# Product order at group ends, residuals and token sums around the second norm, and own buffers for later modulation chunks, in a one-core diffusion block

## The chip, the core and the metric

The kernel runs on one core of a Trainium2 chip. Its engines are TensorE (PE; its weight loads are shown as PEld), VectorE (DVE), ScalarE (ACT), GpSimd (POOL) and SyncE (SP), which issues most DMAs on one in-order queue. The metric is the device time of one execution in microseconds, the median of several runs.

## The reference

One layer of a hybrid backbone on 512 latent tokens of width 2048, with 256 context tokens that only feed the states of the scans. All is in 32-bit floats. Cut to what matters:

```python
mod = c_act @ w_mod + b_mod                 # six vectors of 2048: shift, scale, gate, twice
h = rmsnorm(x, g_norm1) * (1 + sc1) + sh1
z = h @ w_in                                # 4 GLA heads and 4 mLSTM heads: q, k, v, gates
x = x + gt1 * merge_groups(gla(z), mlstm(z), gates, w_out)
h2 = rmsnorm(x, g_norm2) * (1 + sc2) + sh2
u_gate, u_val = split(h2 @ w_up)            # 2 x 5504
g = conv3x3_depthwise(u_gate on an 8 x 64 grid) + conv_b
x = x + gt2 * ((silu(g) * u_val) @ w_down)
out = rmsnorm(x, g_final)
```

## The kernel before

Activations lie transposed: 16 tiles of 128 channels by 512 tokens. Every large product is made of three: a 32-bit operand is split into a high part that ScalarE casts (L89) and a low remainder that VectorE subtracts (L90), and `mm3` adds high x high, high x low and low x high. `load_split` brings a block of weights (128 x 1024 floats, 512 KB) by a DMA on SP's queue into one of four raw buffers (`wraw`, L166) and splits it into one of two high and two low buffers. PSUM has six large banks (`acc`) and two small ones (`psb`) that turn.

The stages follow each other so:

- Projections for the eight heads, those of heads 0 and 1 together at the start; after that, while head h is scanned (`stages`: GLA for h below 4, mLSTM above), the projection for head h+1 runs in between (`project_steps`, 8 loads), and the mixture is written out by hand through `weave`: a stage yields the number of microseconds that it wants covered and gets as many steps of products. While the last head is scanned, the first gate unit (`ga0`) takes the projection's place. TensorE's order in these stages is the program's. In an mLSTM head the products `pg` come first, each in a small bank that ScalarE's exponentials (tile `ed`, L829) read; GpSimd cuts triangles out of `ed` (L832, the selects); then come `cst`, `s` and `po`, whose results are evicted as `dn` and `ob`.
- Three more gate units (`ga1` to `ga3`) and four output units (`wo`), each of 8 loads, 4 blocks and 96 matmuls for a block.
- The second norm: `residual` adds gate x product to x (L957), `square` squares on ScalarE (L964) and adds into a running sum on VectorE, the last two tiles staying apart; `token_rstd` adds these sums over the channels with matmuls against a column of ones (`ps_rms`, L976), takes the root and spreads it (`rb_rms`, L983).
- The up and down projections. Four of the 43 blocks of 128 features run as plain products (`up_two`, tile `u`); the other 39 by `up_seven`: seven products of half size in place of eight, in banks `x`, `w` and `v`. Product 6 of a step is held back as `last` and runs inside the next step, behind its product 0, so that its bank is free by then; at the end of a group it runs at once. After every seventh step or so a group of the down projection (`down_block`, tile `dn`) runs, six in all.
- The last norm, with the same helpers.

Four of the six modulation vectors (regions 2 to 5) aren't needed before the first residual. They are worked out on VectorE, ScalarE and GpSimd beside the products, as a list of fillers that `load_split` takes from: `rate[0]` is added to a credit at each load, and each whole credit takes a filler. For each of 4 regions and 4 blocks, `mod_fillers` lists 8 chunks, 2 empty fillers and an end. A chunk (`mod_chunk`) loads 512 KB (`raw_m`, L248), sums one half on VectorE (L257) and scales the other on ScalarE (L258) for GpSimd to add (L259). The end (`mod_end`, tile `mc`, L268) adds over the channels with four small matmuls in a small bank, in program order on TensorE. `modraw[0]` is the pool that chunks take their tile from: the four weight buffers until the second gate unit, then four tiles of their own. `rate[0]` is 2 on the last five loads of the projections for heads 4 to 7, 2 in the first gate unit and 2.25 after it.

Of the kernel before, what the change touches and what calls it, by code (L numbers as in the profile page):

```python
# [11 lines left out]
F32 = mybir.dt.float32  # L12
# [6 lines left out]
P = 128  # L19
D = 2048  # L20
KT = D // P
# [48 lines left out]
def block_kernel(ctx: ExitStack, tc: tile.TileContext, a: dict, out: bass.AP):  # L70
# [88 lines left out]
    rate, credit = [0], [0]  # L159
    modraw = [wraw]  # L160

# [82 lines left out]
    def mod_chunk(region, n, kp, parts):  # L244

        name = f"m{region}_{n}_{kp}"
        raw = modraw[0].tile([P, 2, T], F32, name=f"raw_{name}", tag="raw")
        nc.sync.dma_start(raw, a["w_mod2"][region - 2, n, kp])  # L248
        if kp == 0:
            parts += [sum_tile(i, name) for i in range(2)]  # L250
        dv, po = parts
        ce, co = (csil[:, 2 * kp + i : 2 * kp + i + 1] for i in range(2))
        if kp == 0:
            V.tensor_scalar(out=dv, in0=raw[:, 0, :], scalar1=ce, scalar2=None, op0=ALU.mult)
            S.activation(po, raw[:, 1, :], AF.Copy, scale=co)  # L255
        else:
            V.scalar_tensor_tensor(out=dv, in0=raw[:, 0, :], scalar=ce, in1=dv, op0=ALU.mult, op1=ALU.add)  # L257
            S.activation(raw[:, 1, :], raw[:, 1, :], AF.Copy, scale=co)  # L258
            G.tensor_tensor(out=po, in0=po, in1=raw[:, 1, :], op=ALU.add)  # L259
        if kp == KP - 1:  # L260
            G.tensor_tensor(out=po, in0=po, in1=dv, op=ALU.add)
# [671 lines left out]
    rp = pool(st_3, "rp")  # L933
    modraw[0] = pool(st_3, "mraw3", 4)
    rate[0] = 2.25
    for g in range(4):
# [22 lines left out]
    def square(k, sums, pl, tag, sl=slice(0, T)):  # L959

        n = sl.stop - sl.start
        first = not sums
        sq = pl.tile([P, n], F32, name=f"sq{tag}{k}", tag=f"{tag}s" if first else f"{tag}{k}" if k >= KT - 2 else tag)
        S.activation(sq, x2[k][:, sl], AF.Square)  # L964
        if first or k >= KT - 2:
            sums.append(sq)
        else:
            add(sums[0], sums[0], sq)

    def token_rstd(sums, pl, name, n=T):  # L970

        nj = n // P
        ps = psb(f"ps_{name}", (P, nj))
        for j in range(nj):
            for i, sq in enumerate(sums):
                PE.matmul(ps[:, j : j + 1], sq[:, P * j : P * j + P], cst[:, C_ONE : C_ONE + 1],  # L976
                          start=(i == 0), stop=(i == len(sums) - 1))
        var, scr, r = (pl.tile([P, nj], F32, name=f"{t}_{name}", tag=t) for t in ("rs1", "rs2", "rs3"))
# [137 lines left out]

    def up_seven(f, pending):

# [28 lines left out]
        pad, val = pads[f % 2], vtile(f)  # L1147
        product(0, a11, x, True)
        with tc.high_priority():
            S.copy(p1, x)  # L1150
        pending()
        product(1, a12, w, True)
        with tc.high_priority():
            add(a11, s1, a11)
            add(a12, a12, a11)
        with tc.high_priority():
            add(pad[:, 1 : ROWS // 2 + 1, 1 : GW + 1], rows(w), rows(p1))
        product(3, s1, v, True)
        with tc.high_priority():
            S.copy(p5, v)  # L1160
        product(2, a11, x, False)
        with tc.high_priority():
            S.copy(u2, x)
        product(5, a12, v, False)
        with tc.high_priority():
            add(pad[:, ROWS // 2 + 1 : ROWS + 1, 1 : GW + 1], rows(v), rows(u2))
        product(4, s3, x, False)
        with tc.high_priority():
            neg_add(val[:, hi], x, p5)

        def last():
            product(6, a22, x, False)
            with tc.high_priority():
                S.activation(val[:, lo], x, AF.Copy, scale=-1.0)
            conv(f, pad, val)

        return last

# [22 lines left out]
    for f in range(FIRST, NF):  # L1201
        last = up_seven(f, last)
        if f == NF - 1 or len(todo) > 1 and f > todo[0][-1]:
            last()
            last = lambda: None
        if len(todo) > 1 and f > todo[0][-1]:
# [144 lines left out]
```

## Time and profile before

| what | us |
|---|---|
| median of three runs (lowest, highest) | 2542.25 (2541.1, 2545.07) |
| the profiled execution's own time | 2540.94 |
| its span, first to last instruction | 2539.2 |
| TensorE busy | 2459.1 |
| VectorE busy | 1666.5 |
| ScalarE busy | 1023.7 |
| GpSimd busy | 301.2 |

The granted clock has a mean of 0.990 over the span. In a row of the trace come start, length, engine, line, operation, tiles (out <- in), shapes and count; in brackets the idle time of the engine before it and what ended that. A row of waits names who waited for what, the total, the number of times and the longest. Matmul ends are modelled, so distances between starts are surer than lengths.

### The profile page before, as it was taken

The page shows a single profiled execution, that of the slowest core. Times are in us where ns is not written, and L with a number is a line of the kernel's source. Part 1 is how long each engine was busy: PE and PEld are TensorE (multiplying, and loading weights), DVE is VectorE, ACT ScalarE, POOL GpSimd, SP SyncE. Part 2 cuts the span into 40 slices and gives each one's busy share as a digit, 9 for nine tenths or more (in the row PEclk, how much of TensorE's full clock was granted, in tenths as well). Part 3 has the DMA queues.
Part 4 walks back from the last instruction along what each step waited for, and adds up shares of the span by engine and source line. Part 5 has one row for each costly group of instructions (what it writes and reads, how often), then busy time and mean ns, then how long its engine had stood idle before and what let it go on. Part 6 is the DMA issues. An engine that isn't in the chain of part 4 may idle for free.

```text
span 2539.2 us, 39245 instructions
## 1 busy us (share of the span) xinstructions
PE 2459.1 (97%) x15758; PEld 2212.8 (87%) x15758; DVE 1666.5 (66%) x2375; ACT 1023.7 (40%) x1559; POOL 301.2 (12%) x263
## 2 busy tenths in 40 slices
PE   5998999999999999999999999999999999999998
PEld 4887899888987887888898999899899889989987
DVE  6566765553435567666895597489479649937974
ACT  4224543333323444443553354245245325424552
POOL 0000000111222444540000000000000000000000
PEclk9999999999999999998999999999999999999999
DMA  8851012213334667773566676677577666756661
GB/s 316 301 201 50 26 43 83 67 63 113 117 109 157 224 240 273 269 257 100 150 164 187 207 191 168 207 202 186 182 209 189 191 203 183 197 197 173 172 205 67
DMA packets 141638, 434.12 MB, mean 171 GB/s; under 512 B 16144, under 2 KB 20496, under 8 KB 141456
## 3 DMA queue, kind: packets, MB, share of 16 engines
q1 hardware_dynamic: 129072, 390.20, 45.0%
q0 software_dynamic: 11232, 40.90, 9.3%
q8 instruction: 123, 2.02, 0.3%
q10 hardware_dynamic: 1152, 0.52, 0.1%
q14 instruction: 59, 0.48, 0.1%
HBM read 402.20 MB, written 29.36 MB: 170 GB/s over the span
## 4 chain that ended last, share of the span: by engine, by line
PE 61%; issue 2%; DMA 2%; DVE 2%; ACT 1%; POOL 1%; SPq 0%; DVEq 0%; POOLq 0%; ACTq 0%
PE dn L95 18%; PE x L95 17%; PE v L95 9%; PE wo L95 6%; PE w L95 4%; PE u L95 4%; DMA raw_m<-in_w_mod 2%; PE ga L95 2%; PE dl L95 1%; DVE sum_m L257 1%; POOL sum_m L259 1%; DVE yT L83 0%; PE mc L268 0%; DVE yTl L90 0%; PE po L95 0%
## 5 line engine op out<-in xcount | busy, mean ns | idle before, releaser
L89 ACT CAST hi_q<-q 128x1024 fp32r<-128x1024 f32 x195 | 205.1, 1052 | 296.0 <-PE v L95 78.3
L95 PE MATMUL dn<-gh,hi_d 128*128 128x512 f32 x656 | 256.2, 391 | 6.4 <-ACT hi_d L89 6.4
L90 DVE TENSOR_TENSOR lo_q<-q,hi_q 128x1024 fp32r<-128x1024 f32 x195 | 238.1, 1221 | 33.3 <-ACT hi_q L89 33.3
L1081 DVE SCALAR_TENSOR_TENSOR cv<-pad,cwt,cv 128x512 f32<-128x512 f32 x344 | 256.7, 751 | 3.6
L95 PE MATMUL dn<-gl,hi_d 128*128 128x512 f32 x656 | 255.6, 390 | 0.0
L95 PE MATMUL dn<-gh,lo_d 128*128 128x512 f32 x656 | 255.4, 389 | 0.0
L259 POOL TENSOR_TENSOR sum_m<-sum_m,raw_m 128x512 f32<-128x512 f32 x112 | 177.4, 1584 | 410.8 <-ACT sum_m L255 226.4
L89 ACT CAST hi_d<-raw_d 128x1024 fp32r<-128x1024 f32 x92 | 88.1, 958 | 290.6 <-PE dn L95 243.5
L90 DVE TENSOR_TENSOR lo_d<-raw_d,hi_d 128x1024 fp32r<-128x1024 f32 x92 | 102.1, 1110 | 143.7 <-ACT hi_d L89 143.6
L257 DVE SCALAR_TENSOR_TENSOR sum_m<-raw_m,csil,sum_m 128x512 f32<-128x512 f32 x112 | 113.6, 1014 | 110.6 <-DMA raw_m<-in_w_mod 110.0
L258 ACT ACTIVATE raw_m<-raw_m,csil 128x512 f32<-128x512 f32 x112 | 80.9, 724 | 179.8 <-DMA raw_m<-in_w_mod 174.0
L95 PEld LDWEIGHTS dn<-gh,hi_d 128*128 128x128 f32 x656 | 123.2, 188 | 33.1 <-ACT hi_d L89 7.6
L95 PE MATMUL a<-hi_h,hTh 128*128 128x256 f32 x512 | 150.8, 295 | 0.0
L95 PE MATMUL a<-hi_h,hTl 128*128 128x256 f32 x512 | 145.5, 284 | 0.0
L95 PE MATMUL a<-lo_h,hTh 128*128 128x256 f32 x512 | 145.4, 284 | 0.0
L95 PEld LDWEIGHTS dn<-gl,hi_d 128*128 128x128 f32 x656 | 123.2, 188 | 25.4
L95 PEld LDWEIGHTS dn<-gh,lo_d 128*128 128x128 f32 x656 | 123.2, 188 | 25.2
L1121 POOL DMA_DIRECT2D spareh<-in_w_up x39 | 33.9, 870 | 746.2 <-DMA spareh<-in_w_up 746.1
L90 DVE TENSOR_TENSOR lo_h<-raw_h,hi_h 128x1024 fp32r<-128x1024 f32 x64 | 80.3, 1255 | 49.0 <-ACT hi_h L89 48.5
L89 ACT CAST hi_h<-raw_h 128x1024 fp32r<-128x1024 f32 x64 | 67.1, 1048 | 106.3 <-PE a L95 90.4
L95 PE MATMUL a<-hTh,hi_h 128*128 128x512 f32 x256 | 106.7, 417 | 1.6 <-ACT hTh L89 1.6
L95 PE MATMUL ga<-hTh,hi_ga 128*128 128x512 f32 x256 | 104.2, 407 | 0.0
(390 smaller groups left out, 7503.1 us busy)
## 6 DMA issues: line engine op xcount, KB each, us to landing
raw_m<-in_w_mod SPq DMA_DIRECT2D x192, 512.0 KB, 5.2
q<-in_w_up SPq DMA_DIRECT2D x117, 512.0 KB, 5.0
raw_d<-in_w_down SPq DMA_DIRECT2D x72, 512.0 KB, 4.7
raw_h<-in_w_heads SPq DMA_DIRECT2D x64, 512.0 KB, 3.6
sparel<-in_w_up SPq DMA_DIRECT2D x39, 512.0 KB, 5.0
spareh<-in_w_up SPq DMA_DIRECT2D x39, 512.0 KB, 3.5
sparel<-in_w_up POOLq DMA_DIRECT2D x39, 512.0 KB, 5.7
spareh<-in_w_up POOLq DMA_DIRECT2D x39, 512.0 KB, 6.2
```

Source lines behind the costliest of these rows:

```text
L89: S.copy(hi, x)
L90: return V.tensor_tensor(out=lo, in0=x, in1=hi.bitcast(F32), op=ALU.subtract).ins
L95: ins = PE.matmul(*args, **kw)
L257: V.scalar_tensor_tensor(out=dv, in0=raw[:, 0, :], scalar=ce, in1=dv, op0=ALU.mult, op1=ALU.add)
L258: S.activation(raw[:, 1, :], raw[:, 1, :], AF.Copy, scale=co)
L259: G.tensor_tensor(out=po, in0=po, in1=raw[:, 1, :], op=ALU.add)
L1081: V.scalar_tensor_tensor(out=t3, in0=src, scalar=w, in1=t3, op0=ALU.mult, op1=ALU.add)
L1121: eng.dma_start(q, a["w_up"][f - FIRST, i, j].rearrange("p k c -> p (k c)"), **kw)
```

## The change

- `modraw[0]` is now a function that gives tiles from a list of places in turn (`slots`). From the scan of head 4 on, chunks take the tiles `sc` and `qi` of the GLA scans, which no mLSTM head uses; from the second gate unit on they have six tiles instead of four.
- The rate is 1.25 on all eight loads of the projections for heads 5 to 7 and of the first gate unit, and 2.3 after that.
- In the output units all four residuals of a unit come before its four squares. For the second norm the last four squares stay apart instead of two, and `token_rstd` goes over sums outside and token blocks inside, in both norms.
- The first product with the second norm's root is made in two halves.
- `up_seven` keeps its order 0, (6 of the step before), 1, 3, 2, 5, 4 inside a group; in a group's last step the order is 0, (6 of the step before), 1, 2, 3, 4, 5, 6.

```diff
-    modraw = [wraw]
+    def slots(*places):
+        turn = [0]
+        def take(name):
+            pl, tag = places[turn[0] % len(places)]
+            turn[0] += 1
+            return pl.tile([P, 2, T], F32, name=name, tag=tag)
+        return take
+    modraw = [slots((wraw, "raw"))]
...
-        raw = modraw[0].tile([P, 2, T], F32, name=f"raw_{name}", tag="raw")
+        raw = modraw[0](f"raw_{name}")
...
-            rate[0] = 2 if h >= H and kp >= 3 else 0
+            rate[0] = 1.25 if h > H else 2 if h == H and kp >= 3 else 0
...
     for h in range(1, 2 * H):
+        if h == H:
+            modraw[0] = slots((wk, "sc"), (wk, "qi"))
...
-            rate[0] = 2
+            rate[0] = 1.25
...
-    modraw[0] = pool(st_3, "mraw3", 4)
-    rate[0] = 2.25
+    modraw[0] = slots((pool(st_3, "mraw3", 6), "raw"))
+    rate[0] = 2.3
...
-        sq = pl.tile([P, n], F32, name=f"sq{tag}{k}", tag=f"{tag}s" if first else f"{tag}{k}" if k >= KT - 2 else tag)
+        own = k >= KT - (4 if n == T else 2)
+        sq = pl.tile([P, n], F32, name=f"sq{tag}{k}", tag=f"{tag}s" if first else f"{tag}{k}" if own else tag)
...
-        for j in range(nj):
-            for i, sq in enumerate(sums):
+        for i, sq in enumerate(sums):
+            for j in range(nj):
                 PE.matmul(ps[:, j : j + 1], sq[:, P * j : P * j + P], cst[:, C_ONE : C_ONE + 1],
-                          start=(i == 0), stop=(i == len(sums) - 1))
+                          start=(i == 0 and j == 0), stop=(i == len(sums) - 1), skip_group_check=True)
...
                 residual(x2[k], k, accs[i], modc[2])
-                square(k, sums2, rp, "sq")
                 nc.sync.dma_start(x2d[k], x2[k])
+            for i in range(4):
+                square(4 * n + i, sums2, rp, "sq")
...
-            mul(t, t, r2)
+            for sl in (slice(0, TH), slice(TH, T)) if k == 0 else (slice(0, T),):
+                mul(t[:, sl], t[:, sl], r2[:, sl])
...
+        steps = [(0, a11, x, lambda: S.copy(p1, x)), (1, a12, w, c11), (2, a11, x, lambda: S.copy(u2, x)),
+                 (3, s1, v, lambda: S.copy(p5, v)), (4, s3, x, lambda: neg_add(val[:, hi], x, p5)), (5, a12, v, c12),
+                 (6, a22, x, lambda: S.activation(val[:, lo], x, AF.Copy, scale=-1.0))]
...
+        step(0)
         pending()
+        step(1)
         with tc.high_priority():
             add(a11, s1, a11)
             add(a12, a12, a11)
...
+        for n in (2, 3, 4, 5) if final else (3, 2, 5, 4):
+            step(n)
+        if final:
+            end()
+            return lambda: None
+        return end
```

More of the change, by code (lines that the diff above doesn't have):

```diff
@@ L1147, in up_seven, with c11, c12, step @@
         pad, val = pads[f % 2], vtile(f)
-        product(0, a11, x, True)
-        with tc.high_priority():
-            S.copy(p1, x)
+        def c11():
+            add(pad[:, 1 : ROWS // 2 + 1, 1 : GW + 1], rows(w), rows(p1))
+        def c12():
+            add(pad[:, ROWS // 2 + 1 : ROWS + 1, 1 : GW + 1], rows(v), rows(u2))
+        steps = [(0, a11, x, lambda: S.copy(p1, x)), (1, a12, w, c11), (2, a11, x, lambda: S.copy(u2, x)),
+                 (3, s1, v, lambda: S.copy(p5, v)), (4, s3, x, lambda: neg_add(val[:, hi], x, p5)), (5, a12, v, c12),
+                 (6, a22, x, lambda: S.activation(val[:, lo], x, AF.Copy, scale=-1.0))]
+        def step(n):
+            m, src, o, after = steps[n]
+            product(m, src, o, m in (0, 1, 3))
+            with tc.high_priority():
+                after()
+        def end():
+            step(6)
+            conv(f, pad, val)
+        step(0)
         pending()
-        product(1, a12, w, True)
+        step(1)
         with tc.high_priority():
```

29 lines of the change are left out of this document (3 added, 26 removed).

## The prediction

> **What bounds the kernel now.** I read the page's busy totals and granted clock first, then busy time by stage, then TensorE's own waits, and last the order of instructions at each place where TensorE stood idle.
>
> ```profile
> PE 2459.1 (97%) x15758; PEld 2212.8 (87%) x15758; DVE 1666.5 (66%) x2375; ACT 1023.7 (40%) x1559; POOL 301.2 (12%) x263
> 535.00:775.00 240.00, 239.98 (x1385) 213.21 (x1383) 96.58 (x218) 77.31 (x139) 44.08 (x40) 1.00 0.33 110
> 775.00:842.00 67.00, 60.94 (x260) 49.28 (x261) 32.18 (x69) 26.10 (x47) 18.43 (x19) 0.95 0.39 136
> 842.00:1002.00 160.00, 154.73 (x696) 126.75 (x694) 107.24 (x108) 76.07 (x103) 74.33 (x46) 1.00 0.74 259
> 1002.00:1167.00 165.00, 164.89 (x742) 136.74 (x742) 98.42 (x106) 65.24 (x84) 65.84 (x41) 0.99 0.68 239
> 1167.00:1180.00 13.00, 8.09 (x37) 7.39 (x38) 6.60 (x16) 4.98 (x12) 1.24 (x2) 0.59 0.51 174
> 1300.00:1400.00 100.00, 98.92 (x635) 89.87 (x634) 69.26 (x85) 36.91 (x48) 4.34 (x5) 1.00 0.66 191
> 2400.00:2500.00 100.00, 98.94 (x567) 87.49 (x567) 68.42 (x95) 50.66 (x81) 6.63 (x9) 1.00 0.45 148
> ```
>
> The columns of a stretch are its length, then busy time of TensorE, its weight loads, VectorE, ScalarE and GpSimd, then the granted clock. TensorE is the bound: a gain must come out of its idle time or its slow clock. The mLSTM heads (535 to 775) leave it 0.02 us idle; the end of head 7 and the first gate unit (775 to 842) leave 6.06; the other gate units 5.27, the output units 0.11, the second norm 4.91, and each of six group ends in the up stage about 1.06 (first and last shown). All lie where the diff works.
>
> **Part A, group ends.** At the end of a group product 6 follows product 4, and both accumulate in bank x:
>
> ```profile
> 1347.05 0.28 PE L95 MATMUL x<-bt2h,lo_q 128*128 128x256 f32 x1
> 1348.14 0.42 DVE L1042 SCALAR_TENSOR_TENSOR val<-x,part_p 128x256 f32<-128x256 f32 x1
> 1348.39 0.50 PE L95 MATMUL dn<-gh,hi_d 128*128 128x512 f32 x1 [1.06 <-ACT hi_d L89]
> 1348.73 0.28 PE L95 MATMUL x<-bt3h,hi_q 128*128 128x256 f32 x1
> 1976.42 1.22 DVE L86 TENSOR_TENSOR q<-spareh,q 128x1024 f32<-128x1024 f32 x1
> 1982.05 2.83 PE w L95 x24
> ```
>
> The last matmul of product 4 starts at 1347.05 and the next on TensorE at 1348.39, 1.34 later, where matmuls of this shape follow each other by 2.83 / 24 = 0.12 (last row, product 1 in the chain of work): 1.22 us lost. Product 6 starts only when VectorE has emptied x (1348.14 + 0.42 = 1348.56); the matmul of the down projection in between merely fills. In the new order 0, 1, 2, 3, 4, 5, 6 product 5 lies between them and VectorE's read of x hides behind its 2.8 us. Every other bank is also refilled at least one product after it was read. What could be late next is product 2, now directly behind product 1: it needs the sum in a11. That sum ran at 1976.42, before product 1 of that step began (1982.05), so I expect no new wait. The instructions are otherwise the same, and loads keep their place in SP's and POOL's queues. Gain 6 x 1.22 = **7.3 us**; ends 0 and 8.
>
> **Part B, chunks while mLSTM heads and the first gate unit run.** The page's list of fillers is 4 regions x 4 blocks x (8 chunks + 2 empty + 1 end) = 176. Before, each of four heads takes 2 on each of its last five loads (40), the first gate unit 2 on each of 8 (16), and 120 remain. After, head 4 still takes 10, heads 5 to 7 take 1.25 on each of 8 loads (10 each), the gate unit also 10, and 126 remain. So 6 fillers, about 4 chunks, move from the gate unit to the output units. Every chunk brings a 512 KB DMA on SP's queue, one pass on VectorE and ScalarE and one on GpSimd. Their tiles leave the four raw weight buffers for two idle scratch tiles.
>
> ```profile
> PE mc L268 <- POOL ed L832: 2.5, 1, 2.5
> PE po L95 <- DVE ed L83: 2.3, 1, 2.3
> PE po L95 <- ACT ob L868: 1.3, 1, 1.3
> 773.85 1.13 PE L95 MATMUL pg<-negg,cst 4*128 4x512 f32 x4
> 775.60 1.77 ACT L829 ACTIVATE ed<-pg,acol 128x512 f32<-128x512 f32 x4
> 777.51 1.84 PE L268 MATMUL mc<-cst,sum_m 128*128 128x1 f32 x8 [2.53 <-POOL ed L832]
> 776.70:783.50 6.80, 5.99 (x18) 5.15 (x19) 2.34 (x4) 5.48 (x12) 5.41 (x10) 0.50 0.70 246
> 799.49 0.75 DVE L257 SCALAR_TENSOR_TENSOR sum_m<-raw_m,csil,sum_m 128x512 f32<-128x512 f32 x1 [2.25 <-DMA raw_m<-in_w_mod]
> 802.23 0.70 PE L95 MATMUL po<-c,qs 128*128 128x258 f32 x2 [2.29 <-DVE ed L83]
> ```
>
> These three waits are 2.53 + 2.29 + 1.26 = 6.08. The first is a block's end (mc) on the unit's second load. I read its true holder as the PSUM bank: only two small banks turn, both pg products hold one, and the exponentials still read the first until 775.60 + 1.77 = 777.37; the named GpSimd wait is the nearest later event. During it the clock falls to 0.50 until 783.5, and from 777.5 half of 6.0 us is lost: 3.0. In the new count the end that is filler 43 comes on the unit's fourth load, past pg, among the po products. The second wait is VectorE's queue: a chunk's sum stood 2.25 us for its DMA with the head's own work behind it. In the new count the second and third loads take only empty fillers, so nothing stands there. The third is the head's evictions behind four chunk sums on VectorE; at 1.25 a load there are fewer. In all 9.1 at stake. Against it stands mc in its new place: it needs a bank that a po product has just filled, which by the third wait costs up to 1.3. I take 9.1 - 1.1 = **8.0 us**; ends -24 (the rival below) and 9.1. In heads 5 to 7 I cost the earlier chunks at nothing: only 0.9 of a tile per load is added, VectorE is 40% busy (96.58 of 240) and the cover is TensorE's unbroken work.
>
> **Part C, six buffers in the other gate and output units, rate 2.3.** 126 / 2.3 = 54.8, so the last filler goes on load 55 of 56; before it was 54.
>
> ```profile
> PE wo L95 <- ACT hi_wo L89: 2.2, 1, 2.2
> PE ga L95 <- DVE lo_ga L90: 1.8, 2, 0.9
> PE wo L95 <- DVE lo_wo L90: 1.4, 2, 0.8
> SPq L248 <- POOL sum_m L259: 29.0, 27, 2.3
> 998.84 0.72 ACT L258 ACTIVATE raw_m<-raw_m,csil 128x512 f32<-128x512 f32 x1 [7.01 <-DMA raw_m<-in_w_mod]
> 997.50:1002.50 5.00, 1.98 (x7) 1.08 (x6) 2.27 (x2) 2.61 (x3) 2.73 (x2) 0.95 1.01 402
> 1002.00:1005.40 3.40, 3.30 (x8) 2.66 (x9) 2.08 (x4) 0.72 (x1) 1.17 (x1) 0.50 1.02 413
> 1002.10 0.80 PE L95 MATMUL wo<-yTh,lo_wo 128*128 128x512 f32 x1 [0.82 <-DVE lo_wo L90]
> ```
>
> ScalarE stood 7.01 us for a chunk's DMA, and the cast of the next weights stood behind it: TensorE waits 2.20, then 0.82 for the next weights' second half (last row), then runs 3.4 us at 0.50 (1.7 lost). SP had held chunks back 27 times until GpSimd gave a buffer free, and then the transfers came in one burst at 402 GB/s. Two more buffers let SP issue earlier, while the DMA share over the whole stage is 0.74. 2.2 + 0.8 + 1.7 = 4.7; 0.5 off for chunks that now stand ahead of weights in SP's queue: **4.2 us**. The waits for lo_ga (1.8) and the smaller one for lo_wo (0.6) are VectorE's own load, and stay. Ends 0 and 7.1.
>
> **Part D, second norm.**
>
> ```profile
> 1167.92 0.63 ACT L964 ACTIVATE sqsq<-x 128x512 f32<-128x512 f32 x1
> 1168.60 3.88 PE L976 MATMUL ps_rms<-cst,sqsq 128*128 128x1 f32 x20 [0.77 <-ACT sqsq L964]
> 1172.51 0.16 DVE L155 TENSOR_SCALAR rs_rms<-ps_rms 128x4 f32<-128x4 f32 x1 [3.24 <-PE ps_rms L976]
> 1176.17 1.88 DVE L83 TENSOR_TENSOR x<-x,rb_rms 128x512 f32<-128x512 f32 x3 [2.23 <-PE rb_rms L983]
> 1179.63 0.58 PE L95 MATMUL u<-b00l,hi_u 128*128 128x256 f32 x1 [0.78 <-DVE b00l L80]
> ```
>
> Now 20 passes run behind the last square, 0.19 each. After, five sums in place of three make 40 passes in place of 24, but only 8 need the last square. The other 32 are ready earlier; if they run ahead of it, 12 x 0.19 = 2.3 us goes from the end, and 16 new passes x 0.12 (part E) to 0.19 = 1.9 to 3.0 come in, part of it in idle time. It balances: I take a gain of **0**, ends -1.5 and 2. Residuals before squares: VectorE leaves out two sums that end before the last square. The split first product gives half of 0.63 us earlier to ScalarE, but TensorE then waits for b00l (0.78) behind one more VectorE instruction: 0, ends -0.3 and 0.3.
>
> **Part E, last norm.** The same helper serves it:
>
> ```profile
> 2516.98 1.72 PE L976 MATMUL ps_rmsf<-cst,sqfq 128*128 128x1 f32 x14
> ```
>
> With sums outside, 6 of these 14 passes need the last square: 8 x 0.12 = 1.0 us sooner, but TensorE has the last products left to do; I take **0.5**, ends 0 and 1.
>
> **Sum.** 7.3 + 8.0 + 4.2 + 0 + 0.5 = 20.0 us. The profiled execution took 2540.94 us, 1.74 of it outside the 2539.2 of its span, and gives 2520.9; the median of the three runs, 2542.25, lies 1.3 above it, and gives 2522.
>
> **A rule weighed.** The rows show the clock at half after idle times of 2.53 and 2.20 us, each with thin or broken work before it. The Trainium skill, TensorE: Matmul & The Clock Gate, Part 1 (the HAM clock gate), says that the clock halves after a whole idle window of about 3.4 us, in windows that run free of the program. By that rule neither idle time alone would do it, so curing them need not bring the clock back (rival 1); the trace agrees with the lengths of the slow stretches (6.8 and 3.4) and not with the idle time needed.
>
> **Rivals.** (1) The clock falls in those places anyhow, since pg and the po products are thin work: 3.0 + 1.7 of the sum go, 2527. For it: the slow stretch begins in the wait; against: pg runs in heads 4 to 6 too, and the clock there is 1.00. (2) The buffers are not the hold: VectorE's and ScalarE's order is, as the lo_ga waits show, and new waits appear in the units: half of B and all of C go, 2530. (3) The new order of products only moves the wait, to product 2 for its weights: A goes, 2529. This is the case that the change doesn't do what it says at the group ends. (4) Both (2) and (3): 2537, no change. (5) Slower: two tiles are too few. SP is one queue, and a chunk that waits for its tile holds the weights behind it; the tile comes free after GpSimd's sum, which stands in line behind the heads' selects.
>
> ```profile
> POOL ed L832 <- ACT ed L829: 123.5, 16, 57.0
> ```
>
> GpSimd stood up to 57.0 us for such a select. If each of the four weaves then lost what the one at 777 lost (2.53 + 3.0 = 5.5), it is 22 us against A, C and E of 12.0: 2552; it decides from 3.0 us a weave. Against: a head has 240 / 3 = 80 us for 10 fillers, so a tile has two loads to come free, and 240 us with 0.02 idle show large cover. (6) Everything cured, the lo waits and D at its good end too: 7.3 + 9.1 + 7.1 + 2 + 1 = 26.5, 2516.
>
> **How the numbers follow.** The forecast 0.37; (1) 0.10, (2) 0.20, (3) 0.10, (4) 0.05, (5) 0.05, (6) 0.13. Faster by over 0.2% (5.1 us, about what a measurement can tell) holds in the forecast, (1), (2), (3) and (6): 0.90; no change 0.05; slower 0.05. The range 2511 to 2533 takes in these five with the bounds of D around (6) and (2) and leaves out (4) and (5).
>
> **What would show it.** A: TensorE 100 of 100 in the stretches with group ends, no gap before product 6. B: no idle time above 1.5 us between 770 and 842, clock 1.00. C: 842 to 1167 with under 3 us idle and no ScalarE wait of 7 us for a chunk. D: under 20 passes behind the last square, and VectorE's first step on their sum within 3 us of the square's end (before: 1172.51 - 1168.55 = 3.96). It would be wrong if heads 5 to 7 show idle time, or if the gate units' waits for weights stay at their present sum.

## The result and the profile after

| | before | after |
|---|---|---|
| median (lowest to highest), us | 2541.64 (2537.02 to 2547.41) | 2547.73 (2543.82 to 2551.64) |
| profiled execution's own time, us | 2540.94 | 2548.32 |
| its span, us | 2539.2 | 2546.6 |

The two kernels ran 20 times each, in turns. The ratio is 1.002, with a 95% interval of 1.0013 to 1.0027: the changed kernel is slower by about 6 us, where 20 us less was forecast.

The table splits the span by the first matmuls of the stages (a reading of the starts in the trace: a head begins with its first `pg` product, head 7 ends where the second gate unit begins, the output units end with their last matmul; a gate or output unit has 192 matmuls, 48 for a block). The stretch ahead of head 4 is untouched by the change, and in the thirteen runs that share its code it varies from 526.0 to 532.4; the sums below leave it out. Each stage is read from one trace. In the runs below that share a stage's code, the old heads agree within 0.1 us, but the three changed heads together lose 10.4 to 12.7, head 7 with the first gate unit takes 69.1 and 72.3 as it was before, and the changed output units take 191.0 to 194.9.

| stage, us | before | after | difference |
|---|---|---|---|
| start to head 4 | 527.1 | 530.3 | (3.2) |
| head 4 | 82.3 | 84.9 | 2.6 |
| head 5 | 82.3 | 87.1 | 4.8 |
| head 6 | 82.1 | 87.4 | 5.3 |
| head 7 with the first gate unit | 69.1 | 61.1 | -8.0 |
| gate units 2 to 4 | 137.7 | 139.9 | 2.2 |
| output units | 185.9 | 193.7 | 7.8 |
| last output product to first up product | 11.0 | 7.8 | -3.2 |
| the four plain up blocks | 92.3 | 92.9 | 0.6 |
| up and down groups | 1228.0 | 1219.7 | -8.3 |
| tail of the down projection (tile `dl`) and last norm | 41.3 | 41.7 | 0.4 |

12.7 lost in the heads, 8.0 won behind them, 10.0 lost in the gate and output units, 3.2 won at the norm, 8.3 won in the up and down groups: +4.2 with the two small ones, and +7.4 with the start, as the spans say.

First the page of the changed kernel and its stretches by stage, with the columns as before (the last two are the busy share of the DMA engines and GB/s):

```profile
PE 2459.2 (97%) x15774; PEld 2207.9 (87%) x15774; DVE 1652.9 (65%) x2374; ACT 1024.3 (40%) x1559; POOL 292.3 (11%) x263
530.00:790.00 260.00, 249.68 (x1414) 218.49 (x1414) 92.14 (x217) 79.13 (x146) 40.95 (x47) 1.00 0.30 97
790.00:851.00 61.00, 58.86 (x261) 47.02 (x258) 28.54 (x65) 26.46 (x47) 14.22 (x16) 1.00 0.41 139
851.00:991.00 140.00, 136.74 (x618) 112.35 (x618) 90.48 (x93) 64.04 (x87) 64.00 (x40) 1.00 0.71 251
991.00:1185.00 194.00, 187.29 (x852) 153.76 (x851) 110.37 (x124) 79.26 (x104) 75.73 (x49) 0.99 0.69 243
1185.00:1198.00 13.00, 8.46 (x42) 7.73 (x42) 9.58 (x24) 5.73 (x12) 1.12 (x2) 0.63 0.37 120
1300.00:1400.00 100.00, 99.82 (x702) 93.02 (x702) 78.28 (x97) 42.35 (x57) 6.08 (x7) 1.00 0.65 187
2400.00:2500.00 100.00, 100.00 (x605) 89.60 (x604) 71.70 (x94) 49.83 (x75) 8.29 (x10) 1.00 0.50 158
```

TensorE's busy total is what it was (2459.2 against 2459.1), so the loss is idle time. Heads 4 to 6, which left 0.02 us idle, now leave 260 - 249.68 = 10.32. The slow clock at the first gate unit is gone (1.00 against 0.95). The two stretches with a group end, which left 1.08 and 1.06 us idle, now leave 0.18 and none.

TensorE's waits of the changed kernel, in the heads (530 to 790) and in the gate and output units (842 to 1175); a row gives the total, the times and the longest:

```profile
PE po L95 <- DVE dn L875: 2.7, 1, 2.7
PE po L95 <- DVE ob L882: 2.5, 2, 1.4
PE s L95 <- DVE ed L83: 1.7, 1, 1.7
PE yt L100 <- DVE ob L589: 1.4, 1, 1.4
PE po L95 <- ACT ob L880: 1.2, 2, 0.6
...
PE wo L95 <- DVE lo_wo L90: 6.7, 5, 2.3
PE ga L95 <- DVE lo_ga L90: 3.3, 4, 1.5
```

In the heads TensorE waits for the head's own evictions on VectorE and ScalarE (`dn`, `ob`, `ed`), and for no weights. In the units it waits for the low parts of weights, VectorE's work too, 10.0 us in all; before, its waits there came to 5.4 (2.2 for a high part, 1.8 + 1.4 for low parts).

The longest of the waits in the heads, in the timeline of head 6:

```profile
723.86 0.75 DVE L269 SCALAR_TENSOR_TENSOR sum_m<-raw_m,csil,sum_m 128x512 f32<-128x512 f32 x1 [1.38 <-DMA raw_m<-in_w_mod]
724.77 0.16 DVE L877 TENSOR_TENSOR dn<-po,dn 128x1 f32<-128x1 f32 x1
724.77 1.28 POOL L271 TENSOR_TENSOR sum_m<-sum_m,raw_m 128x512 f32<-128x512 f32 x1 [3.25 <-ACT raw_m L270]
727.81 0.75 DVE L269 SCALAR_TENSOR_TENSOR sum_m<-raw_m,csil,sum_m 128x512 f32<-128x512 f32 x1 [2.88 <-DMA raw_m<-in_w_mod]
728.47 0.15 DVE L878 RECIPROCAL dn<-dn 128x1 f32<-128x1 f32 x1
729.36 0.67 PE L95 MATMUL po<-c,qs 128*128 128x258 f32 x2 [2.66 <-DVE dn L875]
```

An eviction is three steps on `dn`. Between the second (724.77) and the third (728.47) stands a chunk's sum (L269) that waits 2.88 us for its transfer; VectorE takes its queue in order, the bank stays full, and the next `po` product comes 2.66 us late. From the first `ed` step of a head to its last `ob` VectorE ran 1, 0 and 1 chunk steps in heads 4, 5 and 6 before; now 5, 8 and 7, with 5.6, 8.3 and 10.8 us of waiting ahead of them (counted from the trace).

One wait in the output units, in the timeline:

```profile
1005.73 1.22 DVE L90 TENSOR_TENSOR lo_wo<-raw_wo,hi_wo 128x1024 fp32r<-128x1024 f32 x1
1012.37 0.75 DVE L269 SCALAR_TENSOR_TENSOR sum_m<-raw_m,csil,sum_m 128x512 f32<-128x512 f32 x1 [0.98 <-DMA raw_m<-in_w_mod]
1012.63 3.87 POOL L271 TENSOR_TENSOR sum_m<-sum_m,raw_m 128x512 f32<-128x512 f32 x2
1013.04 2.32 DVE L90 TENSOR_TENSOR lo_wo<-raw_wo,hi_wo 128x1024 fp32r<-128x1024 f32 x1
1014.35 2.14 POOL L271 TENSOR_TENSOR sum_m<-sum_m,raw_m 128x512 f32<-128x512 f32 x1
1015.41 0.50 PE L95 MATMUL wo<-yTh,lo_wo 128*128 128x512 f32 x1 [1.39 <-DVE lo_wo L90]
```

Two things hold the split here: a chunk's sum that stood directly ahead of it, and GpSimd's additions. The split at 1005.73 took 1.22 us, the same split at 1013.04, begun while GpSimd added, took 2.32. The third row merges two additions, of which the second is the one at 1014.35 that the fifth row shows alone, so the first ended by then. From there 1.22 us lead to 1015.57, and the split ended at 1015.36: it ran, near enough, only when the addition was over. The second addition, begun at 1014.35, then took 2.14 us where a lone one takes 1.28 (at 724.77 above). Of the eight waits over 0.25 us for low parts in these units, seven have a chunk's sum directly ahead of the split, and in four the split took 2.31 or 2.32 us.

By groups, GpSimd's additions, the chunk sums and the splits of these units (busy, mean ns of one, then the idle time ahead and what ended most of it):

```profile
L271 POOL TENSOR_TENSOR sum_m<-sum_m,raw_m 128x512 f32<-128x512 f32 x79 | 125.2, 1585 | 192.6 <-ACT sum_m L267 151.5 <-ACT raw_m L270 18.2 <-DMA x2d<-x 17.6
L269 DVE SCALAR_TENSOR_TENSOR sum_m<-raw_m,csil,sum_m 128x512 f32<-128x512 f32 x78 | 74.2, 952 | 72.3 <-DMA raw_m<-in_w_mod 72.0
L90 DVE TENSOR_TENSOR lo_wo<-raw_wo,hi_wo 128x1024 fp32r<-128x1024 f32 x32 | 45.5, 1422 | 9.7 <-ACT hi_wo L89 9.7
```

The sums wait 72.0 us for transfers, and all three run longer than alone (1.28, 0.75 and 1.22).

Last, the end of the first group in the up stage, in the timeline (the last matmul of product 4, VectorE's read of its bank, the last of product 5, the first and the last of product 6, the down projection):

```profile
1359.51 0.28 PE L95 MATMUL x<-bt2h,lo_q 128*128 128x256 f32 x1
1359.83 0.42 DVE L1059 SCALAR_TENSOR_TENSOR val<-x,part_p 128x256 f32<-128x256 f32 x1 [0.27 <-PE x L95]
1362.34 0.28 PE L95 MATMUL v<-b1h,lo_q 128*128 128x256 f32 x1
1362.45 0.28 PE L95 MATMUL x<-bt3h,hi_q 128*128 128x256 f32 x1
1365.16 0.28 PE L95 MATMUL x<-bt3h,lo_q 128*128 128x256 f32 x1
1365.28 0.39 PE L95 MATMUL dn<-gh,hi_d 128*128 128x512 f32 x1
```

Product 6 starts 0.11 us behind product 5; VectorE emptied bank x at 1360.25, 2.2 us earlier. And the second norm, behind the last square:

```profile
1185.64 0.63 ACT L979 ACTIVATE sqsq<-x 128x512 f32<-128x512 f32 x1
1186.32 1.05 PE L991 MATMUL ps_rms<-cst,sqsq 128*128 128x1 f32 x8 [0.72 <-ACT sqsq L979]
1187.41 0.16 DVE L155 TENSOR_SCALAR rs_rms<-ps_rms 128x4 f32<-128x4 f32 x1 [0.44 <-PE ps_rms L991]
```

Eight passes stand behind the last square in place of twenty, and VectorE's first step comes 1187.41 - 1186.27 = 1.14 us after it (before: 3.96).

### The profile page after: what moved, and what is told of

Its sections match the earlier page's. It is cut to its first block, busy times and chain, and to the rows that moved or that the text cites. A ratio compares the mean times of both kernels' runs of the same rounds, so it can differ in the third digit from the quotient of the medians.

```text
span 2546.6 us, 39267 instructions
## 1 busy us (share of the span) xinstructions
PE 2459.2 (97%) x15774; PEld 2207.9 (87%) x15774; DVE 1652.9 (65%) x2374; ACT 1024.3 (40%) x1559; POOL 292.3 (11%) x263
## 4 chain that ended last, share of the span: by engine, by line
PE 64%; issue 5%; DMA 4%; POOL 3%; DVE 2%; ACT 1%; SPq 0%; POOLq 0%; DVEq 0%; ACTq 0%
PE dn L95 18%; PE x L95 17%; PE v L95 9%; PE a L95 5%; PE w L95 4%; DMA raw_m<-in_w_mod 4%; PE u L95 4%; POOL sum_m L271 2%; PE ga L95 2%; PE wo L95 2%; PE dl L95 1%; PE po L95 1%; POOL sum_m L273 0%; DVE lo_wo L90 0%; DVE lo_ga L90 0%
## 5 line engine op out<-in xcount | busy, mean ns | idle before, releaser
L271 POOL TENSOR_TENSOR sum_m<-sum_m,raw_m 128x512 f32<-128x512 f32 x112 | 170.0, 1518 | 395.2 <-ACT sum_m L267 226.5
L269 DVE SCALAR_TENSOR_TENSOR sum_m<-raw_m,csil,sum_m 128x512 f32<-128x512 f32 x112 | 104.3, 931 | 111.4 <-DMA raw_m<-in_w_mod 110.8
L95 PE MATMUL wo<-yTh,lo_wo 128*128 128x512 f32 x256 | 101.3, 396 | 6.7 <-DVE lo_wo L90 6.7
```

The lines of the kernel that those rows point to most:

```text
L95: ins = PE.matmul(*args, **kw)
```

## The experiments

Ratios are to the kernel before, run in turns on the same chip, with 95% intervals.

**Group ends alone.** The kernel before with the new order of products and nothing else.

```diff
-    def up_seven(f, pending):
+    def up_seven(f, pending, final):   # as in the changed kernel
```

> The kernel before with the new order of products at the six group ends, and nothing else of the change. Theory (the ends are worth what the idle time there was): the stretch from the first seven-product step to the last loses 6 x 1.22 to 1.4 = 7.3 to 8.5 us, 2533 to 2534 us beside 2541.6, ratio 0.9967. Rival (TensorE only waits somewhere else, at the start of the down groups or for the weights of product 2): under 2 us, 2540 to 2542.

Measured: 2535.83 against 2542.65 us, 0.9968 (0.9954 to 0.9982). The up and down groups took 1220.0 in place of 1228.0; the other stages stayed within 0.9, but for head 7 with the first gate unit, 72.3 in place of 69.1 with the same code. Part A is worth its 8 us, and the loss of the whole lies elsewhere.

**Which half of the change in the heads costs.** The changed kernel, with in turn: both old in heads 5 to 7 (rate and tiles), the old tiles alone, the old rates alone.

```diff
-            rate[0] = 1.25 if h > H else 2 if h == H and kp >= 3 else 0
+            rate[0] = 2 if h >= H and kp >= 3 else 0        # first and third
-        if h == H:
+        if h == 2 * H - 1:                                  # first and second
             modraw[0] = slots((wk, "sc"), (wk, "qi"))
```

> The changed kernel with the chunks of heads 5 to 7 as before: 2 on each of the last five loads, in tiles of the weight buffers; the first gate unit keeps 1.25 and its two tiles. Both theories of the heads (place: the chunks' sums now stand on VectorE ahead of a head's own evictions during its first loads; tiles: two tiles make the loads late) expect the three heads to go back from 84.9, 87.1 and 87.4 us to 82.3 each: 12.5 us less than the changed kernel, 2535. Rival (the heads lost time for another reason, or the loss moves to the gate unit): 2545 to 2548.

> The changed kernel with its new rate of 1.25 on all loads of heads 5 to 7, but the chunks there in tiles of the four weight buffers; the two scratch tiles serve the first gate unit alone. Theory place: the heads stay slow, about 87 us each, 2546 to 2549. Theory tiles: they go back to about 82.3, 2535.

> The changed kernel with the rate of before in heads 5 to 7 (2 on the last five loads), but the chunks in the two scratch tiles. Theory place: the heads are back at about 82.3 us each, 2535. Theory tiles: they stay at 85 to 87 or get slower, since 2 a load must pass through two tiles, 2547 or more.

| | heads 4, 5, 6 | us | ratio |
|---|---|---|---|
| changed kernel | 84.9, 87.1, 87.4 | 2547.73 | 1.002 (1.0013 to 1.0027) |
| both old | 82.3, 82.3, 82.2 | 2535.41 | 0.997 (0.9959 to 0.9982) |
| new rates, old tiles | 83.4, 82.8, 84.3 | 2537.33 | 0.9973 (0.996 to 0.9986) |
| old rates, new tiles | 82.3, 82.3, 82.1 | 2535.0 | 0.9963 (0.9949 to 0.9978) |

The loss comes with the rates, but the rates alone cost 3.8 us, and it takes the tiles to make that 12.7; the tiles alone cost nothing. So neither half is the cause by itself. The first gate unit kept its gain in all three. With the new rates and old tiles TensorE's waits in the heads are of the same kind:

```profile
PE po L95 <- DVE ed L83: 1.9, 1, 1.9
PE po L95 <- ACT ob L880: 1.7, 2, 0.8
PE mc L280 <- POOL ed L844: 0.2, 1, 0.2
```

Three chunk steps run inside each head's evictions there, none with the old rates and new tiles, 5 to 8 in the changed kernel: the count goes with the loss. Old tiles are the weight buffers, and a chunk that has to wait for one of them comes late in VectorE's queue; free tiles of their own let the steps run ahead. That is a reading of the order; a later experiment holds the order and nothing else.

**Four tiles in place of six in the gate and output units.**

```diff
-    modraw[0] = slots((pool(st_3, "mraw3", 6), "raw"))
+    modraw[0] = slots((pool(st_3, "mraw3", 4), "raw"))
```

> The changed kernel with four chunk tiles in place of six after the first gate unit, rate 2.3 kept. Its gate units 1 to 3 and output units took 139.9 and 193.7 us, 2.2 and 7.8 more than before. Theory (six tiles let GpSimd fall behind in long bursts, so that VectorE waits for it and its splits run beside it): the two stages return to about 138 and 189 (the second norm's early passes stay among the output units), 2540 to 2541. Rival (the 6 fillers that were moved here, or the rate, are the cause): no less than 139 and 193, 2546 or more.

Measured: 2537.24 against 2542.91 us, 0.9972 (0.9961 to 0.9983). Gate units 2 to 4 went from 139.9 to 137.7, the output units from 193.7 to 186.8: the two more buffers cost some 9 us and cured nothing.

**Running sums in two sets.** VectorE's first step of a block waited 20.3 us in all, 9 times, for GpSimd's last addition of the block before. A second set of tiles for the sums takes that away.

```diff
-        return accp.tile([P, T], F32, name=f"sum{i}_{name}", tag=f"sum{i}")
+        turn2[i] += 1
+        pl, tag = (accp, f"sum{i}") if turn2[i] % 2 == 0 or not sumx else (sumx[0], f"sumx{i}")
+        return pl.tile([P, T], F32, name=f"sum{i}_{name}", tag=tag)
```

> The changed kernel with the chunks' two running sums in two sets of tiles by turns after the first gate unit, so that a block's first chunk need not wait for GpSimd's last addition of the block before. Theory (that wait, 17.7 us on VectorE in 8 times, is what makes the splits of weights late): TensorE's waits for lo_wo and lo_ga, 10.0 us in all, fall to 6 or less, 2543 to 2545. Rival (VectorE's waits for a chunk's DMA, or splits that run beside GpSimd's additions at 2.3 us in place of 1.2): waits stay within 1 us, 2547.

Measured: 2546.1 us, 1.0012 (1.0001 to 1.0022). The wait fell from 20.3 to 2.6, TensorE's waits for low parts only from 10.0 to 9.1 (5.3 and 3.8). That wait isn't the cause.

**The second norm as before** (sums, order of residuals and squares, the unsplit product, and with them the helper that the last norm shares), the rest changed.

> The changed kernel with the second norm and the helper of the token sums as before: squares beside residuals, two sums apart, token blocks outside, the first product whole. Theory (its parts balance): the output units get 3 to 4 us shorter, since 32 of 40 passes ran among their matmuls, and the stretch from the last output matmul to the first up matmul goes from 7.8 back to 11.0; in all within 1.5 us of the changed kernel, 2546 to 2549. Rival (the new norm is a gain): 2550 or more; rival (it is a loss): 2545 or less.

Measured: 2545.14 us, 1.0011 (1.0001 to 1.002). The output units fell to 189.5 and the norm behind them rose to 9.6: what the new norm wins behind the last product it seems to spend ahead of it, where 24 of its 40 passes now run between output products, 0.11 us apart, 2.6 us in all. How much of the fall to 189.5 is the norm isn't shown, since the output units vary by 4 us with the same code. The medians differ by 2.6 us, and the interval overlaps that of the whole change.

**Old rates everywhere, new tiles** (2 on the last five loads of heads 5 to 7 and in the first gate unit, 2.25 after it).

> The changed kernel with the rates of before: 2 on the last five loads of heads 5 to 7, 2 in the first gate unit, 2.25 after that; the chunks there still in the two scratch tiles, and six tiles later. Theory (the first gate unit gains from taking 10 fillers instead of 16): head 7 with this unit returns from 61 to 69 us or more, since 2 a load must pass through two tiles. Theory (the weights' own four buffers are what it gains from): it stays at 60 to 63. The later units take 120 fillers instead of 126: if those 6 are what made them slow, they return to 138 and 189; if the six tiles are, they stay at 140 and 193. In all 2530 to 2543.

Measured: 2542.54 us, 0.9999 (0.9987 to 1.001). Head 7 with the first gate unit came to 67.6, so the gain of 8.0 there is the thinner filling. The output units stayed at 194.2: the six fillers moved into them are not what they lose by; the six tiles are.

**VectorE's order held.** The changed kernel, with every VectorE instruction of a filler kept behind the split of the load that took it.

```diff
-            split(hi, lo, raw)
+            ins = split(hi, lo, raw)
...
-                fillers.pop(0)()
+                with tc.issue_after(ins):
+                    fillers.pop(0)()
```

> The changed kernel with one order added: on VectorE a filler's steps stand behind the split of the load that took the filler. Tiles, rates and loads are the change's. Theory (order: more chunk tiles let chunk steps run ahead in VectorE's queue, past the splits and a head's evictions that TensorE waits for): heads 4 to 6 come from 84.9, 87.1 and 87.4 to 82.3 to 84.3 each, gate units 1 to 3 from 139.9 to 138 or less, output units from 193.7 to 189 or less; in all 2531 to 2535. Rival (the tiles themselves: more loads at once on the DMA engines, or GpSimd's additions beside VectorE's splits): the gate and output units stay within 2 us of 139.9 and 193.7, 2540 or more.

Measured: 2522.67 against 2544.87 us, 0.9918 (0.9906 to 0.9931). Heads 4 to 6 took 81.4, 82.8 and 82.1 with the new rates and the two tiles, with two chunk steps inside each head's evictions and no waiting ahead of them. The waits of TensorE there:

```profile
PE mc L281 <- POOL ed L845: 0.2, 1, 0.2
```

For the heads the order on VectorE is the cause. In the gate and output units the hold alone did little: 139.2 and 193.0. The hold also acts ahead of head 4, where the last loads of head 4's projection already take chunks in the kernel before: up to head 4 the five runs with a hold take 520.8 to 524.5 us and the thirteen others 526.0 to 532.4, and TensorE's waits for the tile `ex` of head 3 there are 1.5 us with the hold, 5.4 before and 6.4 in the changed kernel. So some 5 us of the gain cure a loss that is older than the change.

**The two cures crossed**: four tiles with old head rates, the hold with old head rates, and the hold with four tiles.

> The change without its two costly parts: heads 5 to 7 with 2 a load on the last five loads, four chunk tiles after the first gate unit; kept are the group ends, the gate unit's 1.25 with its two tiles, rate 2.3 and the norms. By the stages measured alone (group ends -8.2, gate unit -8.5, the rest within 1): 2541.6 - 16 = 2525 to 2527, ratio 0.9935. If the parts do not add up, 2530 or more.

> As the kernel with one order added, and with the rate of before in heads 5 to 7; six tiles after the first gate unit. Theory order: heads 82.3 each, and six tiles behind the split do at least as well as four: 2522 to 2527. Rival (six tiles are costly by themselves): 2533 to 2536, as with the rate of before alone.

> The changed kernel with every filler held behind the weight split of its load (as in e9_hold) and four chunk tiles in the gate and output units in place of six. If six tiles cost time by themselves, whatever the order on VectorE: gate units 2 to 4 fall from 139.2 to about 137.5, the output units from 193.0 to about 187, the heads stay at 82.3 each, and the time is 2522.7 - 1.7 - 6 = about 2515, ratio to before 0.989. If the held order has already taken what the tile count costs, the stages stay at 139 and 193 and the time at about 2522, ratio 0.992.

Measured: 2525.34 us, 0.9926 (0.9912 to 0.994); 2524.77, 0.9923 (0.991 to 0.9936); 2517.27, 0.9891 (0.9867 to 0.9916). Under the hold the old and the new head rates give the same (0.9923 and 0.9918). The third, at 135.3 and 188.1 in the units against 139.2 and 193.0 with six tiles, shows that six tiles cost some 9 us in the held order too (3.9 + 4.9), where the expectation of the second had six doing as well as four. Groups of splits in the gate and output units, six tiles held and four tiles held (columns as above):

```profile
L90 DVE TENSOR_TENSOR lo_wo<-raw_wo,hi_wo 128x1024 fp32r<-128x1024 f32 x32 | 51.6, 1614 | 37.3 <-ACT hi_wo L89 36.0 <-DMA raw_m<-in_w_mod 1.3
L90 DVE TENSOR_TENSOR lo_ga<-raw_ga,hi_ga 128x1024 fp32r<-128x1024 f32 x21 | 32.7, 1557 | 20.3 <-ACT hi_ga L89 20.3
```

```profile
L90 DVE TENSOR_TENSOR lo_wo<-raw_wo,hi_wo 128x1024 fp32r<-128x1024 f32 x32 | 45.5, 1423 | 40.1 <-ACT hi_wo L89 40.1
L90 DVE TENSOR_TENSOR lo_ga<-raw_ga,hi_ga 128x1024 fp32r<-128x1024 f32 x20 | 27.8, 1391 | 19.8 <-ACT hi_ga L89 17.5 <-DMA raw_m<-in_w_mod 2.2
```

A split takes 1.61 us on average with six tiles and 1.42 with four, and 1.22 alone. So the next experiments take GpSimd away.

**GpSimd's additions made short**, in the changed order and in the held one. Both kernels leave out 480 of the 512 columns of each second half in gate units 2 to 4 and the output units.

```diff
-            G.tensor_tensor(out=po, in0=po, in1=raw[:, 1, :], op=ALU.add)
+            w = short[0]
+            G.tensor_tensor(out=po[:, 0:w], in0=po[:, 0:w], in1=raw[:, 1, 0:w], op=ALU.add)
...
+    short[0] = 32
```

> The changed kernel with six tiles, but in gate units 2 to 4 and the output units GpSimd adds only the first 32 of 512 columns of each chunk's second half to the running sum; the other columns of that sum are left out. Order and transfers stay. If GpSimd's additions beside the weight splits are what six tiles cost (a split took 2.32 us beside them and 1.22 alone): output units from 193.7 to about 187, gate units from 139.9 to about 138, time about 2539, ratio 0.999. If the chunk sums' place in VectorE's order, or the transfers, are the cause: both stages stay within 1.5 us, time about 2547, ratio 1.002.

> As e13_short_add (the same columns of the sums are left out in the same stages), but with every filler held behind the split of its load. Slow splits (over 1.8 us) were 19 of 56 in e9_hold, 19.4 us above 1.23 us each. If the additions slow the splits and this is what is left there: slow splits under 6, output units from 193.0 to about 187, time about 2516, ratio 0.989. If the transfers of six tiles hold the weights, the splits may be fast but TensorE waits for weights just as long: output units 192 to 193, time about 2522, ratio 0.992.

Measured: 2532.26 us, 0.9955 (0.9938 to 0.9973), and 2511.68, 0.9869 (0.9848 to 0.989). Gate units 2 to 4 came to 135.3 in both, the output units to 185.6 and 183.4: more than the additions had been expected to be worth. In the changed order, by groups:

```profile
L271 DVE SCALAR_TENSOR_TENSOR sum_m<-raw_m,csil,sum_m 128x512 f32<-128x512 f32 x78 | 58.6, 751 | 80.1 <-DMA raw_m<-in_w_mod 80.0
L90 DVE TENSOR_TENSOR lo_wo<-raw_wo,hi_wo 128x1024 fp32r<-128x1024 f32 x32 | 40.1, 1253 | 17.3 <-ACT hi_wo L89 17.3
L90 DVE TENSOR_TENSOR lo_ga<-raw_ga,hi_ga 128x1024 fp32r<-128x1024 f32 x24 | 29.4, 1224 | 8.5 <-ACT hi_ga L89 8.3
```

VectorE still waits 80.0 us for chunks' transfers (72.0 in the changed kernel), and TensorE waits 1.7 us in place of 10.0. A chunk's sum stands directly ahead of 32 of the 55 splits there, as in the changed kernel, so such sums are nearly harmless in these units as long as nothing slows the splits.

**The same sums on VectorE**, nothing left out: one more multiply-add there in place of ScalarE's scaling and GpSimd's addition, and the last addition of a block's two sums there as well, in gate units 2 to 4 and the output units.

```diff
-            S.activation(raw[:, 1, :], raw[:, 1, :], AF.Copy, scale=co)
-            G.tensor_tensor(out=po, in0=po, in1=raw[:, 1, :], op=ALU.add)
+            if allv:
+                V.scalar_tensor_tensor(out=po, in0=raw[:, 1, :], scalar=co, in1=po, op0=ALU.mult, op1=ALU.add)
+            else:                                           # the two lines as they were
...
-            G.tensor_tensor(out=po, in0=po, in1=dv, op=ALU.add)
+            (V if allv else G).tensor_tensor(out=po, in0=po, in1=dv, op=ALU.add)
```

> e9_hold with the whole of each chunk summed on VectorE in gate units 2 to 4 and the output units: the second half by one more multiply-add of 0.75 us in place of ScalarE's scaling and GpSimd's addition; nothing is left out. If GpSimd's additions beside the splits are the cost, gate units 2 to 4 come to about 135.5 and the output units to 183.5 to 186 as in e14_hold_short, and the time to 2512 to 2516, ratio 0.987 to 0.989. If VectorE's extra 45 x 0.75 = 34 us cost as much as GpSimd's neighbourhood did, both stages stay near 139 and 193, time 2522, ratio 0.992.

> The changed kernel with the same sums on VectorE and its order not held. If GpSimd's additions are the cost: gate units 2 to 4 from 139.9 to about 135.5, output units from 193.7 to about 186, time about 2533 as in e13_short_add, ratio 0.996. If chunk steps ahead of the splits on VectorE count as well, twice as many now stand there and wait for their transfer once: both stages within 2 us of 139.9 and 193.7, time about 2547, ratio 1.002.

Measured: 2512.73 against 2543.22 us, 0.9881 (0.9866 to 0.9896), with the hold; 2532.48, 0.9964 (0.9951 to 0.9976), without it. The units came to 135.3 and 183.4 in both. Groups of the first of the two, and its heads (527 to 770) and gate units (830 to 965) by stretches:

```profile
L272 DVE SCALAR_TENSOR_TENSOR sum_m<-raw_m,csil,sum_m 128x512 f32<-128x512 f32 x77 | 57.4, 746 | 0.1
L90 DVE TENSOR_TENSOR lo_wo<-raw_wo,hi_wo 128x1024 fp32r<-128x1024 f32 x32 | 39.1, 1223 | 28.3 <-ACT hi_wo L89 28.3
```

```profile
527.00:770.00 243.00, 242.77 (x1394) 215.48 (x1392) 91.32 (x212) 74.37 (x140) 38.48 (x43) 1.00 0.30 100
830.00:965.00 135.00, 135.00 (x617) 112.29 (x616) 96.48 (x135) 44.30 (x57) 0.00 (x0) 1.00 0.80 276
```

VectorE took on 77 steps of 0.75 us in these units, 57.4 us, but its busy time rose by some 20 only, since its own steps no longer stretch: 96.48 of 135 us in the gate units against 90.48 of 140 in the changed kernel, 125.04 of 185 against 110.37 of 194 in the output units. Of the versions that leave nothing out this is the shortest run here, 1.2% (1.0 to 1.3) under the kernel before; its interval overlaps that of the hold with four tiles.

## Why the prediction was wrong, step by step

- **A, right.** 7.3 forecast, 8.0 measured alone. No new wait at product 2; the shape is as described.
- **B, first half right.** The first gate unit's gain was put at 8.0 and is 8.0 (69.1 to 61.1), the clock there is back at 1.00. That the tenth agrees is luck: with the same code this stage took 59.8 to 63.5 in other runs, and 72.3 in place of 69.1 as it was before. The wait for `mc`, for which 1.1 was set aside, did not come; one of 2.1 us for `dn` is left, over the 1.5 named.
- **B, "In heads 5 to 7 I cost the earlier chunks at nothing", failed: 12.7 us.** The cover named was TensorE's unbroken work and VectorE's 40%. Neither protects an eviction: what counts is what stands ahead of it in VectorE's queue. The same part had read that very wait at 802 ("a chunk's sum stood 2.25 us for its DMA with the head's own work behind it") and did not ask where else the new rates and tiles would put a chunk's sum.
- **C failed, in sign too: 4.2 gain forecast.** The units lost 10.0, of which some 2.6 are the norm's 24 passes (an estimate from their starts) and belong to D; four tiles give 9.1 back (2.2 + 6.9); together that is a little over the loss, within the spread of these stages. The step that failed is "Two more buffers let SP issue earlier", which took the buffers for the whole price: ScalarE's single wait of 7 us fell to 6.3 and TensorE's wait for a high part is gone, but its waits for low parts, behind splits that run beside GpSimd's additions, grew by more. (The stretch 842 to 1002 that the prediction calls the other gate units takes in the output units from 980.7 on, and that wait for a high part lies there.) "The waits for lo_ga (1.8) and the smaller one for lo_wo (0.6) are VectorE's own load, and stay" was wrong twice: they grew from 3.2 to 10.0, and it takes GpSimd's additions to make them, since all but 1.7 go when these go. In the trace before, too, the two splits behind the waits for `lo_ga` took 2.32 and 2.31 us, each begun during an addition of GpSimd.
- **D right, E not to be seen.** D was put at 0: 3.2 won behind the last product, and some 2.6 spent ahead of it. E was put at 0.5, and the last stage shows no gain (41.3 and 41.7; 41.6 in the two other runs with the old order of its passes, 41.4 to 42.5 in those with the new one).
- **The rivals.** (1) fell where it was looked at first: the slow clock at 777 went with its wait. (2) had the right place, the order on VectorE and ScalarE, but as a gain that stays out; it is a loss. (3) fell. (5) had the right sign and heads and the wrong mechanism: no weights wait in the heads, the two tiles do no harm (81.4, 82.8 and 82.1 with the order held), and VectorE's queue is what is held, not SP's. Its 5.5 us a weave came out at 2.6 to 5.3 in three of them. The condition named, "wrong if heads 5 to 7 show idle time, or if the gate units' waits for weights stay", came true in both halves: the units' waits did not even stay, they grew.
- **The clock rule.** The clock went to half once more in the output units, behind 2.34 us without a matmul:

```profile
1036.00:1041.70 5.70, 3.36 (x16) 2.45 (x14) 3.22 (x5) 1.80 (x3) 5.47 (x4) 1.00 0.80 309
1041.70:1045.10 3.40, 3.40 (x8) 2.75 (x9) 2.17 (x4) 1.57 (x2) 2.38 (x2) 0.51 0.59 213
```

  while the wait of 2.66 us in head 6, above, left it at 1.00. The traces show what differs. In each of the 18, the slow stretches begin on a grid of 3.413 us, and all but the last, which the end of the kernel cuts, last whole steps of it. The wait that ends at 1041.70 lay within one step, in which TensorE was busy 31% of the time; the one in head 6 lay across the border of two, busy 70% and 52%. (In the kernel before, the steps with the waits at 777 and 1000 were busy 50% and 21% and slowed it; the one with the wait at 802 was busy 52% and did not.) Over all 18 traces (TensorE's modelled busy time, steps at full clock, without the first and last 40 us) a step busy less than 43% was followed by a slow one 26 times of 26, from 43 to 50% 14 times of 29, from 50 to 60% never in 81; of the busier ones that were, all but one lie in the second norm. So in this kernel about half a step of idle time is enough, if it falls within one step. The rule weighed in the prediction (the Trainium skill, TensorE: Matmul & The Clock Gate, Part 1), a whole idle window of about 3.4 us in windows that run free of the program, agrees with the grid and the length of the slow stretches and not with the idle time needed.

What stays open: why six tiles set more additions beside the wrong splits than four. In the changed order the mean split is as slow with four tiles as with six (1436 and 1422 ns in the output units), and chunk sums stand directly ahead of about as many of the 55 splits (31 and 32, and 30 in the kernel before). What differs is that the waits fall together with them: seven of eight with six tiles, one of three with four. The runs show that the loss needs the additions, not how the tiles set the pattern; the short additions and the sums on VectorE also give chunk tiles back sooner, which no run separates.

## What to carry to other kernels

More buffers for work that can be done at any time do not only take waits away: they let its steps move ahead in the in-order queues of the engines that also do urgent work. So ask of every such step what stands behind it when its transfer is late, and tie it behind the urgent instruction of its own load (here worth some 25 us against the change as it stood, some 5 of them ahead of head 4, where the change did nothing). And price a helper engine by what it does to its neighbour: the same sums done on VectorE alone made the gate and output units 13 to 15 us shorter (332.2 with the hold and 333.6 without, to 318.7), although they added to its busy time.

## What the runs showed of the hardware

The wait of VectorE and GpSimd for each other was not expected at this size. An addition of 128 x 512 floats took 1.28 us on GpSimd alone and 1.59 on average in the units; VectorE's split of 128 x 1024 took 1.22 us with GpSimd quiet and 2.32 where it began during an addition, its multiply-add 0.75 alone and 0.95 on average. The order of starts and ends in the rows at 1013 fits one engine standing still until the other's instruction has ended. So does the split at 1005.73, which began first: it took 1.22 us, and the addition that was issued during it, at 1006.09, took 2.01. The Trainium skill, SBUF — State Buffer, section "SBUF: two separate sides", states that: the shared port pair is "an exclusive lock, not a bandwidth split", held for a whole instruction, also against a VectorE operation with two SBUF inputs; the rows agree, and 1.10 us (2.32 - 1.22) is within the length of one addition. The kernel before had it already: its mean split in the output units was 1344 ns.
